# Attention scores on one core: first unit loaded contiguously and stored in halves, and a looped TensorE program over one 8-bank PSUM tensor

## The chip, the cores and the metric

The kernel runs on one core of a Trainium2 chip. The metric is the device time of one execution in microseconds, given as the median over nine executions. The engines are named as in the profile: PE is TensorE, DVE is VectorE, ACT is ScalarE, POOL is GpSimd, SP is SyncE. SP computes nothing here: it issues transfers to the core's 16 DMA engines.

## The reference

```python
batch, heads, seq, dim = 8, 8, 512, 64          # q, k: float32 [8, 8, 512, 64]
scale = 1.0 / np.sqrt(q.shape[-1])
return (np.einsum('bhqd,bhkd->bhqk', q, k) * scale).astype(np.float32)
```

There are 64 pairs of batch and head. Each one gives a 512 by 512 score matrix from a 512 by 64 query and a 512 by 64 key. The inputs hold 16.78 MB together, the output 67.11 MB.

## The kernel before

**Units and tiles.** The work is cut into four units (`v`, 0 to 3) of two batches each. A unit has a 2.1 MB load of k and one of q. From a unit come four tiles, so there are sixteen (`g`, 0 to 15). A tile is an SBUF buffer of 128 partitions by 2 by 8 by 512 float32 values, 4.19 MB, and is stored with one transfer. The index `x` (0 or 1) of the second dimension is one head of the two on each partition's row, called a half below; each half is 8 matmuls of 128 by 512.

**Buffers.** Three SBUF buffers `big0` to `big2` serve twice: the loads land in them (`xf`, line 58), and after the casts the tiles' results are written into them (`store_buffer`, line 62; tile g uses one of the three in turn). A tile can be filled only once the tile three before it, in the same buffer, has been stored.

**The engines' programs.** They are written out by hand and tied together by semaphores.

- SP (lines 69, 75, 91 to 102) issues the first half of the first k load (ACT issues the second half), then five loads, then the last two loads as buffers come free (`ready`). After that it loops over the tiles: it waits until ACT and DVE have written a tile, then issues its store (line 99). Each buffer has a semaphore of stores, `store_sems[g % 3]`; a store adds 16. At the end it waits for all stores.
- POOL (line 121) casts what was loaded to bf16 and counts `ready` up, once for each load.
- DVE (lines 148, 156) turns keys and queries with 32 by 32 block transposes into `kT` and `qz`: six transposes for one batch (`steps(b)`), which serves two tiles. The transposes of the next batch are laid between the PSUM evictions, by the table `after`.
- PE (line 140) does 256 matmuls. They are unrolled in the instruction stream, two for each of 128 pairs. A pair writes one of four PSUM buffers (`pss`, two banks each) in rotation, and before writing it PE waits until the pair four before has been taken out. At the second matmul of a tile PE also waits until its SBUF buffer is free: on `ready` for the first three tiles, and from the fourth on the semaphore of the store three tiles before.
- ACT and DVE (lines 186, 189) take each pair, 128 by 1024 values, out of PSUM, scale it and write it to the tile's buffer. `takers` says who takes which of the eight pairs of a tile: ACT five, DVE three.

**What the access patterns say.** `k_r`, `q_r` (lines 41, 42) and `out_r` (line 43) describe how DRAM rows lie on the partitions. In `out_r` the partition dimension `(h u)` is one head number and 64 row blocks; these lie one behind the other in DRAM, so that dimension is a single one of 128 steps, of 16 KB each. The store's pattern on the DRAM side is 128 by 2 by 4096 values, on the SBUF side too. The loads' pattern is 32 by 4 by 4096 on the DRAM side (the two half loads: 32 by 4 by 2048) and 128 by 4096 on the SBUF side.

Of the kernel before, what the change touches and what calls it, by code (L numbers as in the profile page):

```python
# [5 lines left out]
def kernel(  # L6
    tc: tile.TileContext,
    q: bass.AP,
    k: bass.AP,
    out: bass.AP,  # L10
):
    nc = tc.nc
    B, H, S, D = q.shape
    scale = 1.0 / (D ** 0.5)
    P = 128
    Q = 32
    UNITS = B // 2
    G = H // 2
    M = P // (2 * H)
    R = S // M  # L20
    J = R // 2
    RO = 8
    U = S // RO
    JJ = J // RO
    PAIRS = RO
    ALL = 2 * B

    f32 = mybir.dt.float32
    bf16 = mybir.dt.bfloat16
    mult = mybir.AluOpType.mult  # L30


    names = ["ready", "zeroed", "pe", "act", "dve"]
    sem = {name: nc.alloc_semaphore(name) for name in names}
    load_sems = [nc.alloc_semaphore(f"load{n}") for n in range(2 * UNITS)]
    halves = [load_sems[0], nc.alloc_semaphore("load0b")]
    store_sems = [nc.alloc_semaphore(f"store{n}") for n in range(3)]

    q_r = q.rearrange("(v b) (x s h) (m j) d -> v (s h m) (b x) (j d)", b=2, x=2, s=2, j=R)
    k_r = k.rearrange("(v b) (x s h) (m j) d -> v (s h m) (b x) (j d)", b=2, x=2, s=2, j=R)
    out_r = out.rearrange("(v b) (x s h) (u i) k -> v s b (h u) x (i k)", b=2, x=2, s=2, i=RO)

    bigs = [nc.alloc_sbuf_tensor(f"big{n}", [P, 2, RO, S], f32)[:] for n in range(3)]
    xb = nc.alloc_sbuf_tensor("xb", [P, 2 * UNITS, J, D, 2], bf16)[:]
    kT = nc.alloc_sbuf_tensor("kT", [P, 2 * G, S], bf16)[:]
    qz = nc.alloc_sbuf_tensor("qz", [P, 2 * G, RO, P], bf16)[:]
    pss = [nc.alloc_psum_tensor(f"ps{n}", [P, 2, S], f32)[:] for n in range(4)]

    xw = xb.rearrange("p n w d e -> p n (w d e)").bitcast(f32).rearrange(
        "p n (w d) -> p n w d", d=D)
    kw = kT.bitcast(f32)
    qw = qz.bitcast(f32)

    def xf(v):
        return bigs[(0, 1, 2, 1)[v]].rearrange("p x i k -> p (x i k)").rearrange(
            "p (x s c) -> p x s c", x=2, s=2)  # L60

    def store_buffer(g):
        return bigs[(0, 2, 1)[g % 3]]

    def rows(v, x):
        return (k_r, q_r)[x][v]

    def load(v, x):
        nc.sync.dma_start(out=xf(v)[:, x].rearrange("p s c -> p (s c)"), in_=rows(v, x)  # L69
                          ).then_inc(load_sems[2 * v + x], 16)  # L70

    for s, queue in enumerate((nc.sync, nc.scalar)):
        first_load = queue.dma_start(
            out=xf(0)[:, 0, s], in_=rows(0, 0)[..., s * R * D // 2:(s + 1) * R * D // 2]
        ).then_inc(halves[s], 16)
        tc.no_tile_sem_insts.add(first_load.ins.name)
    tc.close()
    tc.compile()  # L80


    takers = ["act", "dve", "act", "act", "dve", "act", "dve", "act"]

    def taken(pair):
        g, p = divmod(pair, PAIRS)
        who = takers[p]
        return who, g * takers.count(who) + takers[:p + 1].count(who)


    for n in range(1, 2 * (UNITS - 1)):
        load(n // 2, n % 2)
    for x in range(2):
        nc.sync.wait_ge(sem["ready"], 3 + x)
        load(UNITS - 1, x)
    for g in range(ALL):
        for who in ("act", "dve"):
            nc.sync.wait_ge(sem[who], takers.count(who) * (g + 1))
        nc.sync.dma_start(out=out_r[g // 4, g // 2 % 2, g % 2], in_=store_buffer(g).rearrange("p x i k -> p x (i k)")
                          ).then_inc(store_sems[g % 3], 16)  # L100
    for n in range(3):
        nc.sync.wait_ge(store_sems[n], 16 * len(range(n, ALL, 3)))


    for v in range(UNITS):
        for x in range(2):
            if v or x:
                nc.gpsimd.wait_ge(load_sems[2 * v + x], 16)
            for s in range(2):
                if v == x == 0:  # L110
                    nc.gpsimd.wait_ge(halves[s], 16)
                src = xf(v)[:, x, s]
                dst = xb[:, 2 * v + x]
                if x == 0:
                    src = src.rearrange("p (w e d) -> p w e d", e=2, d=D)
                    dst = dst[:, s * J // 2:(s + 1) * J // 2].rearrange("p w d e -> p w e d")
                else:
                    src = src.rearrange("p (jj e i d) -> p jj e i d", e=2, i=RO, d=D)
                    dst = dst.rearrange("p (i jj) d e -> p jj e i d", i=RO)[
                        :, s * JJ // 2:(s + 1) * JJ // 2]  # L120
                cast = nc.gpsimd.tensor_copy(out=dst, in_=src)  # L121
            cast.then_inc(sem["ready"], 1)


    pe = nc.tensor
    for pair in range(ALL * PAIRS):
        g, p = divmod(pair, PAIRS)
        n, i = g % 4 * 2 + p // 4, p % 4 * 2
        for w in range(2):
            if w == 0 and pair >= 4:  # L130
                who, count = taken(pair - 4)
                pe.wait_ge(sem[who], count)
            elif w == 0 and pair == 0:
                pe.wait_ge(sem["zeroed"], 2)
            if p == 0 and w == 1:
                if g < 3:
                    pe.wait_ge(sem["ready"], (2, 6, 8)[g])
                else:
                    pe.wait_ge(store_sems[g % 3], g // 3 * 16)
            ins = pe.matmul(out=pss[pair % 4][:, w, :], lhsT=qz[:, n, i + w], rhs=kT[:, n],  # L140
                            start=True, stop=True)
        ins.then_inc(sem["pe"], 1)

    def turn_keys(b, y):
        s = b % 2 * 2 * Q
        return nc.vector.transpose(  # L148
            out=kw[2 * y * Q:2 * (y + 1) * Q, b % 2 * G:(b % 2 + 1) * G].rearrange(
                "d g (m w) -> d w m g", w=J),  # L150
            in_=xw[s:s + 2 * Q, b // 2 * 2, :, y * Q:(y + 1) * Q])

    def turn_queries(b, y, h):
        s = (b % 2 * 2 + h) * Q
        d = (2 * y + h) * Q
        return nc.vector.transpose(  # L156
            out=qw[d:d + Q, b % 2 * G:(b % 2 + 1) * G, :, h * Q:(h + 1) * Q].rearrange(
                "d g i (m jj) -> d i jj m g", jj=JJ),
            in_=xw[s:s + Q, b // 2 * 2 + 1, :, y * Q:(y + 1) * Q].rearrange(
                "p (i jj) d -> p i jj d", i=RO))  # L160

    def steps(b):
        nc.vector.wait_ge(sem["ready"], b // 2 * 2 + 1)
        yield turn_keys(b, 0)
        yield turn_keys(b, 1)
        nc.vector.wait_ge(sem["ready"], b // 2 * 2 + 2)
        for y in range(2):
            for h in range(2):
                yield turn_queries(b, y, h)

    nc.vector.memset(qz, 0.0).then_inc(sem["zeroed"], 1)  # L171
    nc.vector.wait_ge(sem["zeroed"], 1)
    for last in steps(0):
        pass
    last.then_inc(sem["zeroed"], 1)


    after = {(0, 1): 1, (0, 4): 1, (0, 6): 2, (1, 1): 2}
    coming = iter(())
    for pair in range(ALL * PAIRS):  # L180
        g, p = divmod(pair, PAIRS)
        o = store_buffer(g)[:, p // 4, p % 4 * 2:p % 4 * 2 + 2, :]
        ps = pss[pair % 4]
        if takers[p] == "act":
            nc.scalar.wait_ge(sem["pe"], pair + 1)
            nc.scalar.mul(out=o, in_=ps, mul=scale).then_inc(sem["act"], 1)  # L186
        else:
            nc.vector.wait_ge(sem["pe"], pair + 1)
            nc.vector.tensor_scalar(out=o, in0=ps, scalar1=scale, scalar2=None, op0=mult  # L189
                                    ).then_inc(sem["dve"], 1)  # L190
        if p == 0 and g % 2 == 0 and g // 2 + 1 < 2 * UNITS:
            coming = steps(g // 2 + 1)
        for _ in range(after.get((g % 2, p), 0)):
            next(coming, None)


# [28 lines left out]
```

## Time and profile before

| | us |
|---|---|
| median of 9 executions | 201.64 (201.42 to 201.73) |
| the profiled execution, its own time | 201.71 |
| its span, first to last instruction | 200.4 |
| DVE busy | 155.0 |
| PE busy | 86.5 |
| ACT busy | 79.6 |
| POOL busy | 39.1 |

The span is what the trace covers; the execution's own time is 1.3 us longer. Busy times of the engines overlap each other. HBM traffic is 16.78 MB read and 67.11 MB written. The mean time of one instruction of each kind: a matmul 503 ns, an ACT eviction of 128 by 1024 1024 ns, a DVE eviction of the same size 1218 ns, a transpose of the keys 1946 ns and of the queries 2003 ns, a POOL cast 2468 ns. From issue to landing a store takes 15.2 us (median of 16).

### The profile page before, as it was taken

To read this page: it belongs to the slowest core of one execution; us is meant where nothing else is said; L and a number is where in the kernel's file an instruction comes from. 1 tells how busy PE (TensorE), PEld (TensorE's weight loads), DVE (VectorE), ACT (ScalarE), POOL (GpSimd) and SP (SyncE) were. 2 spreads that over 40 slices of the span, in tenths; PEclk is the share of its full clock that TensorE was granted. 3 is DMA by queue.
4 is the path that set the end of the run, shared out by engine and by line. 5 is a ranking of instruction groups with operands and counts; after the bars stand their busy time and mean duration, and the time that the engine had idled before them with its cause. 6 is when DMAs were issued, how large, how long until landed. Compare 5 with 4: busy or idle time off the path is not lost.

```text
span 200.4 us, 784 instructions
## 1 busy us (share of the span) xinstructions
PE 86.5 (43%) x251; PEld 28.3 (14%) x256; DVE 155.0 (77%) x97; ACT 79.6 (40%) x81; POOL 39.1 (19%) x20
## 2 busy tenths in 40 slices
PE   0000075464935492349225745573556247930000
PEld 0000021121311131113112211221122112300000
DVE  2338959995999899989998999899999996740000
ACT  2000036272852475327532942393347344860000
POOL 0489999986000000000000000000000000000000
PEclk9999999575797579856996975597578965885555
DMA  5999999999999999999999999999999999999996
GB/s 201 427 438 442 428 419 419 451 360 432 428 442 425 432 428 442 417 432 428 445 422 430 428 442 425 432 428 442 422 428 435 425 428 435 428 428 419 425 419 278
DMA packets 5652, 83.94 MB, mean 419 GB/s; under 512 B 400, under 2 KB 400, under 8 KB 400
## 3 DMA queue, kind: packets, MB, share of 16 engines
q1 hardware_dynamic: 5504, 82.84, 97.4%
q10 hardware_dynamic: 144, 1.05, 1.2%
q8 instruction: 2, 0.03, 0.1%
q14 instruction: 2, 0.02, 0.0%
HBM read 16.78 MB, written 67.11 MB: 419 GB/s over the span
## 4 chain that ended last, share of the span: by engine, by line
DVE 53%; DMA 17%; PE 8%; POOL 5%; ACT 3%; issue 1%; SPq 1%
DVE qz L156 24%; DVE big L189 18%; DMA big<-in_q_dram 17%; DVE kT L148 12%; PE ps L140 8%; POOL xb L121 5%; ACT big L186 3%; SPq L69 1%
## 5 line engine op out<-in xcount | busy, mean ns | idle before, releaser
L140 PE MATMUL ps<-kT,qz 128*128 128x512 bf16 x251 | 86.5, 503 | 90.7 <-DVE big L189 57.0
L186 ACT ACTIVATE big<-ps 128x1024 f32<-128x1024 f32 x80 | 78.3, 1024 | 96.1 <-PE ps L140 93.6
L189 DVE TENSOR_SCALAR big<-ps 128x1024 f32<-128x1024 f32 x48 | 57.8, 1218 | 11.1 <-PE ps L140 10.7
L156 DVE STREAM_TRANSPOSE qz<-xb 32x1024 f32<-32x1024 f32 x32 | 64.1, 2003 | 1.3 <-POOL xb L121 0.8
L140 PEld LDWEIGHTS ps<-kT,qz 128*128 128x128 bf16 x256 | 28.3, 121 | 148.4 <-DVE big L189 75.1
L121 POOL CAST xb<-big 128x2048 bf16<-128x2048 f32 x16 | 38.9, 2468 | 9.0 <-DMA big<-in_k_dram 7.9
L148 DVE STREAM_TRANSPOSE kT<-xb 64x1024 f32<-64x1024 f32 x16 | 31.1, 1946 | 6.8 <-POOL xb L121 6.4
L171 DVE MEMSET qz<- 128x4096 uint32 x1 | 3.5, 3472 | 3.5 <-PEq L80 3.5
L186 ACT ACT_TABLE_LOAD x1 | 1.3, 1283 | 2.6 <-PEq L80 2.6
L209 POOL MEMSET const-float32-0.0<- 128x1 f32 x1 | 0.1, 98 | 0.2 <-issue 0.2
L209 POOL MEMSET const-bfloat16-1.0<- 128x1 bf16 x1 | 0.1, 101 | 0.0
L209 POOL MEMSET const-uint8-127<- 128x1 uint8 x1 | 0.1, 101 | 0.0
L209 POOL MEMSET const-float32-1.0<- 128x1 f32 x1 | 0.1, 98 | 0.0
## 6 DMA issues: line engine op xcount, KB each, us to landing
out_dram<-big SPq DMA_DIRECT2D x16, 4096.0 KB, 15.2
big<-in_q_dram SPq DMA_DIRECT2D x4, 2048.0 KB, 17.3
big<-in_k_dram SPq DMA_DIRECT2D x3, 2048.0 KB, 14.9
big<-in_k_dram SPq DMA_DIRECT2D x1, 1024.0 KB, 5.7
big<-in_k_dram ACTq DMA_DIRECT2D x1, 1024.0 KB, 10.0
```

The costliest lines, as they stand in the source:

```text
L69: nc.sync.dma_start(out=xf(v)[:, x].rearrange("p s c -> p (s c)"), in_=rows(v, x)).then_inc(load_sems[2 * v + x], 16)
L121: cast = nc.gpsimd.tensor_copy(out=dst, in_=src)
L140: ins = pe.matmul(out=pss[pair % 4][:, w, :], lhsT=qz[:, n, i + w], rhs=kT[:, n], start=True, stop=True)
L148: return nc.vector.transpose(out=kw[2 * y * Q:2 * (y + 1) * Q, b % 2 * G:(b % 2 + 1) * G].rearrange("d g (m w) -> d w m g", w=J), in_=xw[s ...
L156: return nc.vector.transpose(out=qw[d:d + Q, b % 2 * G:(b % 2 + 1) * G, :, h * Q:(h + 1) * Q].rearrange("d g i (m jj) -> d i jj m g", jj=J ...
L171: nc.vector.memset(qz, 0.0).then_inc(sem["zeroed"], 1)
L186: nc.scalar.mul(out=o, in_=ps, mul=scale).then_inc(sem["act"], 1)
L189: nc.vector.tensor_scalar(out=o, in0=ps, scalar1=scale, scalar2=None, op0=mult).then_inc(sem["dve"], 1)
L209: nc = _bacc.Bacc("TRN2", target_bir_lowering=False, num_devices=1)
```

## The change

It has four parts.

1. **The first unit's layout.** For unit 0, `rows` now gives k and q of the first two batches as plain contiguous memory, 128 rows of 4096 values (the two half loads: 128 rows of 2048). A partition is now batch, head and eighth of the sequence, where it was head, eighth, batch and part of the heads. The transposes of the first two batches (`inside(b)`) therefore write their result in another order.
2. **The first unit's stores.** With that layout the two heads of a half are four apart in the output. A half is described by the new pattern `out_0`, in which `h` (2 steps of 4 MB) and `u` (64 steps of 16 KB) are two dimensions that can't be one. Each of tiles 0 to 3 is stored by two transfers, one for each half, of 2 by 64 by 4096 values on the DRAM side and 128 by 4096 on the SBUF side. Each adds 16 to the buffer's semaphore, so such a tile adds 32. Tiles 4 to 15 are stored as before.
3. **PSUM and the evictions.** PSUM is one tensor of 8 banks, and matmul i of a half always writes bank i. A half is taken out in three groups: banks 0 and 1 by DVE, 2 to 4 and 5 to 7 by ACT. There are 32 DVE evictions of 128 by 1024 (were 48) and 64 ACT evictions of 128 by 1536 (were 80 of 128 by 1024). DVE does two transposes after the eviction of three of every four halves, none after the fourth.
4. **PE's loop and the waits.** PE runs a loop of four iterations over four tiles (64 matmuls). [...] the semaphores come in two sets (`act0`, `act1`, `dve0`, `dve1`, `next0`, `next1`), which PE counts down again. Leave for a tile's SBUF buffer no longer comes from the store's own semaphore: SP passes it on. After it has issued tile g's store, SP waits for the store of tile g - 1 (for the buffer of tile g + 2) and adds one to `next0` or `next1`, and only then goes on to tile g + 1.

```diff
+    out_0 = out.rearrange("b (h t x) (u i) k -> b t x h u (i k)", h=2, x=2, i=RO)
     out_r = out.rearrange("(v b) (x s h) (u i) k -> v s b (h u) x (i k)", b=2, x=2, s=2, i=RO)
...
-    pss = [nc.alloc_psum_tensor(f"ps{n}", [P, 2, S], f32)[:] for n in range(4)]
+    ps = nc.alloc_psum_tensor("ps", [P, RO, S], f32)[:]
...
     def rows(v, x):
-        return (k_r, q_r)[x][v]
+        if v == 0:
+            return (k, q)[x][:2].rearrange("b g (m j) d -> (b g m) (j d)", j=R)
+        return (k, q)[x].rearrange(
+            "(v b) (x s h) (m j) d -> v (s h m) (b x) (j d)", b=2, x=2, s=2, j=R)[v]
...
-            out=xf(0)[:, 0, s], in_=rows(0, 0)[..., s * R * D // 2:(s + 1) * R * D // 2]
+            out=xf(0)[:, 0, s], in_=rows(0, 0)[:, s * R * D // 2:(s + 1) * R * D // 2]
...
+    groups = [(0, 2, "dve"), (2, 3, "act"), (5, 3, "act")]
+    share = {"act": 4, "dve": 2}
+    def stored(n, tiles):
+        return sum(32 if g < 4 else 16 for g in range(n, tiles, 3))
...
     for g in range(ALL):
         for who in ("act", "dve"):
-            nc.sync.wait_ge(sem[who], takers.count(who) * (g + 1))
-        nc.sync.dma_start(out=out_r[g // 4, g // 2 % 2, g % 2], in_=store_buffer(g).rearrange("p x i k -> p x (i k)")
-                          ).then_inc(store_sems[g % 3], 16)
+            nc.sync.wait_ge(sem[f"{who}{g // 2 % 2}"], share[who] * (g % 2 + 1))
+        o = store_buffer(g).rearrange("p x i k -> p x (i k)")
+        if g < 4:
+            for x in range(2):
+                nc.sync.dma_start(out=out_0[g // 2, g % 2, x], in_=o[:, x]
+                                  ).then_inc(store_sems[g % 3], 16)
+        else:
+            nc.sync.dma_start(out=out_r[g // 4, g // 2 % 2, g % 2], in_=o
+                              ).then_inc(store_sems[g % 3], 16)
+        for later in ((1, 2) if g == 0 else (g + 2,)):
+            if later < ALL:
+                if later < 3:
+                    nc.sync.wait_ge(sem["ready"], 4 + 2 * later)
+                else:
+                    nc.sync.wait_ge(store_sems[later % 3], stored(later % 3, later))
+                nc.sync.sem_inc(sem[f"next{later // 2 % 2}"], 1)
...
-    for pair in range(ALL * PAIRS):
...
-                    pe.wait_ge(store_sems[g % 3], g // 3 * 16)
-            ins = pe.matmul(out=pss[pair % 4][:, w, :], lhsT=qz[:, n, i + w], rhs=kT[:, n],
-                            start=True, stop=True)
-        ins.then_inc(sem["pe"], 1)
+    takes = {(0, 3): ("next", 2), (1, 3): ("dve", 2 * share["dve"]), (1, 6): ("act", 2 * share["act"])}
+    pe.wait_ge(sem["zeroed"], 2)
+    with pe.Fori(0, ALL // 4):
+        for t in range(4):
+            two, r = divmod(t, 2)
+            for x in range(2):
+                before = (2 * t + x - 1) % 8
+                for i in range(RO):
+                    if i in waits:
+                        who, count = waits[i]
+                        pe.wait_ge(sem[f"{who}{before // 4}"], before % 4 * per_half[who] + count)
+                    elif x == 0 and i == 1:
+                        pe.wait_ge(sem[f"next{two}"], r + 1)
+                    ins = pe.matmul(out=ps[:, i], lhsT=qz[:, 2 * t + x, i], rhs=kT[:, 2 * t + x],
+                                    start=True, stop=True)
...
+    def inside(b):
+        return "g m" if b < 2 else "m g"
...
-                "d g (m w) -> d w m g", w=J),
+                f"d g (m w) -> d w {inside(b)}", w=J),
...
-    after = {(0, 1): 1, (0, 4): 1, (0, 6): 2, (1, 1): 2}
...
+    for g in range(ALL):
+        for x in range(2):
+            for i, rows_, who in groups:
+                count += 1
+                engine = nc.scalar if who == "act" else nc.vector
+                engine.wait_ge(sem["pe"], count)
+                o, src = store_buffer(g)[:, x, i:i + rows_], ps[:, i:i + rows_]
...
+            for _ in range(2 if (g % 2, x) != (1, 1) else 0):
+                next(coming, None)
```

## The prediction

> **What bounds the kernel now.** I read the page's DMA rows first, then busy time by stretches, then SP's own waits, and last the queues' packet counts.
>
> The page (slices of 5.0 us; the busy row in tenths, then what was moved), and its section on queues:
>
> ```profile
> PE 86.5 (43%) x251; PEld 28.3 (14%) x256; DVE 155.0 (77%) x97; ACT 79.6 (40%) x81; POOL 39.1 (19%) x20
> DMA  5999999999999999999999999999999999999996
> GB/s 201 427 438 442 428 419 419 451 360 432 428 442 425 432 428 442 417 432 428 445 422 430 428 442 425 432 428 442 422 428 435 425 428 435 428 428 419 425 419 278
> DMA packets 5652, 83.94 MB, mean 419 GB/s; under 512 B 400, under 2 KB 400, under 8 KB 400
> ...
> q1 hardware_dynamic: 5504, 82.84, 97.4%
> q10 hardware_dynamic: 144, 1.05, 1.2%
> ...
> HBM read 16.78 MB, written 67.11 MB: 419 GB/s over the span
> ```
>
> The DMA engines are full in 38 of 40 slices, while no compute engine is busy more than 77% of the span. The transfers are the bound. Busy time by stretches (PE, weight loads, DVE, ACT, POOL, each with its count; then clock, DMA share, GB/s):
>
> ```profile
> 5.00:36.00 31.00, 6.67 (x17) 2.30 (x17) 21.67 (x13) 5.01 (x5) 27.43 (x12) 0.99 1.01 432
> 36.00:46.00 10.00, 5.61 (x15) 1.95 (x15) 9.91 (x6) 4.90 (x5) 9.12 (x5) 0.67 0.98 393
> ...
> 106.00:126.00 20.00, 11.34 (x31) 3.46 (x32) 18.99 (x13) 9.80 (x10) 0.00 (x0) 0.70 1.01 431
> 126.00:146.00 20.00, 10.96 (x32) 3.42 (x32) 18.97 (x14) 9.80 (x10) 0.00 (x0) 0.70 1.01 431
> ```
>
> With a share of 1.01 the 16 engines move 431 GB/s, so one moves 431/16 = 26.94 GB/s. Each carries 83.89/16 = 5.243 MB, which takes 194.6 us. The other 200.4 - 194.6 = 5.8 us are the start, the last landing, and a dip at 36 to 46 us worth (431 - 393)/431 x 10 = 0.9 us.
>
> The chain of waits names DVE for 53%, because DVE's instructions follow each other without gaps. It runs 97% full over two tiles (49.86 to 69.75 us in the chain, six evictions of 1.22 and six transposes of about 2.0 are 19.2 of 19.9). Two tiles' stores are 8.39 MB, or 19.5 us at 431 GB/s. DVE and DMA are level, with the loads' backlog in front of the DMA engines, and SP's waits show it:
>
> ```profile
> SPq L98 <- DVE big L189: 142.5, 16, 11.2
> SPq L69 <- POOL xb L121: 21.6, 2, 17.3
> SPq L102 <- DMA out_dram<-big: 21.6, 2, 19.3
> ```
>
> SP waits for DVE before each store, yet after the last store it still waits 19.3 us for the landing: two tiles were queued. Faster compute alone can therefore win only part of the 5.8 us.
>
> **The packet counts** carry most of what follows. Queue q1 has 16 stores of 128 x 2 rows and 8 loads of 128 rows, 4096 + 1024 = 5120 data packets. The 384 left are 24 transfers x 16. Queue q10 has one half load: 144 = 128 + 16. So each transfer of before ends with 16 small packets, one for each of 16 engines, and each engine has a sixteenth of its bytes.
>
> [...] The trace agrees for what it has: 128 against 128 and 32 against 128 both give 16, the 16 small packets. It has no transfer with a small outer dimension. [...]
>
> **The change part by part.**
>
> *Stores of tiles 0 to 3.* Before, 4 transfers with outer dimensions 128 and 128. After, 8 of 2.10 MB with 2 on the DRAM side and 128 on the SBUF side. [...] Bytes on each of these two:
> - loads: 16.78/16 = 1.049 MB;
> - tiles 0 to 3: 4 x 4.194/2 = 8.389 MB (were 1.049);
> - tiles 4 to 15: 12 x 4.194/16 = 3.146 MB.
>
> The sum is 12.583 MB, 2.4 times 5.243. At 26.94 GB/s that is 467.1 us. One of these tiles is 2.097 MB on each of the two engines, 77.8 us, where it took 9.7.
>
> Do the two engines ever run dry? The loads keep them to about 43 us (the last one landed at 43.4). Tile 0's store was issued at 35.9 and will queue behind them. Then SP issues tile 1, waits until tile 0 is stored, issues tile 2, and so on: one tile is always queued while one moves, and a tile is computed in about 10 us (tile 0 from the first matmul at 26.4 to its store at 35.9), long before 77.8 are over. I count tile 0 landing near 121, tile 1 near 199, 2 near 276 and 3 near 354. Tile 4 is issued at about 276, when tile 2 has landed. The other 14 engines finish their share of it in 10 us, the two do so only after tile 3, near 364. Then eleven tiles at 9.7 us follow in the same way. The overheads of before remain without the dip, 5.8 - 0.9 = 4.9 us: 467.1 + 4.9 = 472.0 us of span. The execution's time stood 1.3 above its span: 473.3. Its own time, 201.71, is 0.07 above the median of the runs, so 473.
>
> The unknown is the speed of one engine when fourteen are idle. Below: [...] the best slice of before, 451/16 = 28.2, gives 452. Above: the worst full stretch, 393/16 = 24.6, gives 512 + 6.2 = 518. I take 26.94, since it holds over a hundred microseconds, and each engine's packets were 16 KB rows before and stay so.
>
> *SP's added waits.* SP waits for tile g - 1's landing before it goes on to tile g + 1; behind it stand only the stores. In 16-engine work a store was issued 15.2 us before its landing and the tile before the previous one had landed 2 x 9.7 - 15.2 = 4.2 us earlier: the wait would be over already, cost 0, at most the chain's usual hop of 0.05 us, under a queue of 9.7 us. Under two engines this wait holds tile 2's store to tile 0's landing, with tile 1 still queued: 0 as well. Without that queued tile it would cost a compute time, 10 us a tile.
>
> *Contiguous first loads.* The same bytes in rows of 8 and 16 KB. Issues took 0.63 and 0.54 us. Gain 0 to 0.6 us at the start of tile 0, which is behind the loads on the DMA queues; I take 0. *Eight transposes with other steps:* 1.95 and 2.0 us each as before; were they half as long again, 12 x 1.0 us, the DMA queue of 77.8 us a tile covers it.
>
> *Evictions.* DVE loses 16 x 1.218 = 19.5 us. ACT goes from 80 x 1.024 to 64 of 1.5 times the size, at most 64 x 1.54 = 98.3 us. PE has the same 256 matmuls. *PE's loop:* three branches taken; [...] hidden for the same reason. All of it: 0.
>
> **Rivals.**
>
> - *Stores spread over 16 engines all the same* (not slower). For it: every transfer of before, also 32 against 128, ran on 16. [...] Then bytes per engine are as before, 194.6 us. DVE over two tiles: three halves of 1.22 + 4.0 and a fourth bound by PE and ACT near 3.5, 19.2 us, against 19.9 before and 19.5 for the DMA. Some of the dip and tail would go: 0.9 + 0.3, about 200.5. It decides as soon as k is 8 or more: at k = 8 the two-fold share of four tiles, 1.05 MB, adds 39 us to eight of the engines, still slower; so only k = 16 ends here.
> - *Each half on its own pair of engines*, four in all. For it: two transfers for a tile. [...] 1.049 + 4.194 + 3.146 = 8.389 MB, 311.4 + 6.2 = 318 us.
> - *The new PSUM handoff or the loop becomes the bound* with 16-engine stores: if the fourth half took 5.2 us too, 20.9 us for two tiles, 8 x 1.0 more, 209. It needs the first rival's condition.
>
> **How the numbers follow.** Two engines: 0.92, 473 us, own range 440 to 510. Sixteen: 0.05, of it 0.02 faster, 0.015 within, 0.015 slower. Four: 0.03. A measurement of this kernel tells a change of about 0.2% from none. Slower: 0.92 + 0.03 + 0.015 = 0.965; within 0.015; faster 0.02. The range of the likeliest case is the whole one, cut at the top to 510, since the 393 GB/s stretch mixed a gap into its mean.
>
> **What would show it.** Packets in q1: with k = 2 they are 8 x 130 + 12 x 272 + 8 x 144 = 5456, with k = 16 5568; under 512 B 352 against 464. From about 45 to 350 us the DMA row should stand at one tenth with some 54 GB/s, but for tile 4's burst on the other engines near 276, and then, for tiles 4 to 15, move at 431 or below. PE, ACT and DVE are idle for some 70 us between tiles. From issue to landing the half stores of tiles 0 to 2 should take 45 to 155 us. A DMA row that stays at nine makes this wrong at its first step; one tenth at another rate than 54 GB/s makes only the size wrong.

## The result, and the profile after

| | before | after |
|---|---|---|
| median, us | 201.6 (201.29 to 201.9, 30 runs beside it) | 474.36 (474.31 to 474.72, 10 runs) |
| profiled execution: own time / span, us | 201.71 / 200.4 | 474.3 / 473.0 |

The changed kernel takes 2.354 times as long as the kernel before, with a 95% interval of 2.352 to 2.355. Here and below two executions that were much slower than their like are left out: one of 378.3 us of the kernel before and one of 214.33 us of the kernel that stores one head from each of two queues.

These are lines of the page of the changed kernel. The 40 slices are now 11.8 us each, so a digit covers more than twice the time that it covered before.

```profile
PE 92.3 (20%) x252; PEld 29.5 (6%) x256; DVE 137.1 (29%) x81; ACT 90.1 (19%) x65; POOL 38.9 (8%) x20
...
DMA  8995111111111111111111163111118999999993
GB/s 331 434 427 252 55 53 55 53 55 53 55 53 55 53 55 53 55 53 55 53 55 53 53 269 139 54 54 54 54 53 364 423 425 440 421 425 421 439 424 168
DMA packets 5602, 83.90 MB, mean 177 GB/s; under 512 B 352, under 2 KB 352, under 8 KB 352
...
q1 hardware_dynamic: 5456, 82.84, 41.4%
q10 hardware_dynamic: 144, 1.05, 0.7%
```

The bytes are the same. What is new is the long row of ones: from the fifth slice to the thirtieth the 16 DMA engines are busy for one tenth on average and move 53 to 55 GB/s. The one exception is a burst at slices 24 and 25. The packet counts say why. Queue q1 had 5504 packets, 384 of them the small ones that end a transfer on each engine. With eight half stores in place of four stores, sixteen engines for each would have given 5568. It has 5456, and 352 small packets where there were 400: twelve stores and eight loads with 16 each on q1, one load with 16 on q10, and eight half stores with 2 each.

Busy times by stretches of the changed kernel (start and end, length, then PE, weight loads, DVE, ACT, POOL with counts, clock, DMA share, GB/s):

```profile
46.00:120.00 74.00, 4.71 (x17) 1.34 (x18) 10.81 (x7) 6.27 (x5) 1.92 (x1) 0.57 0.13 54
...
200.00:275.00 75.00, 4.23 (x12) 1.16 (x9) 8.59 (x5) 5.22 (x4) 0.00 (x0) 0.52 0.13 54
275.00:290.00 15.00, 5.46 (x16) 1.66 (x16) 6.50 (x4) 5.48 (x4) 0.00 (x0) 0.73 0.74 289
290.00:350.00 60.00, 0.00 (x0) 0.00 (x0) 0.00 (x0) 0.00 (x0) 0.00 (x0) 0.50 0.13 54
...
400.00:430.00 30.00, 16.81 (x50) 5.27 (x48) 27.15 (x17) 17.34 (x13) 0.00 (x0) 0.83 1.01 429
```

A share of 0.13 is two of sixteen. The two move 54 GB/s, so each moves 27.0. In 290 to 350 us no computing engine has one instruction. At 275 tile 4, which sixteen engines share, goes out: the other fourteen do their part (289 GB/s in the mean of that stretch) and are idle again. From 356 us on all sixteen work as before.

Two pieces from the chain of waits (start, length, what), and one row of SP's own waits:

```profile
48.08 29.66 SPq L106
77.74 0.05 issue
77.79 38.02 SPq L106
115.81 4.11 another core or an unknown queue
```

```profile
SPq L117 <- DMA out_dram<-big: 178.6, 13, 79.6
SPq L119 <- DMA out_dram<-big: 20.7, 2, 19.5
```

Line 106 is the issue of a half store. Tile 1's first half is issued at 48.08 us, and SP stands in that instruction for 29.66 us; in the second half it stands for 38.02 us. A store of before took 0.372 us to issue. Up to 300 us SP's waits for landings at line 117 are only 16.0 us in all; the longest, 79.6 us, is for tile 3 after tile 4's issue. The chain goes on after the tiles' landings: 119.9 us for tile 0, then 197.7, 275.4 and 356.0.

### The profile page after: what moved, and what is told of

The parts are those of the page before. It is cut to its first block, busy times and chain, and to the rows that moved or that the text cites. A ratio compares the mean times of both kernels' runs of the same rounds, so it can differ in the third digit from the quotient of the medians.

```text
span 473.0 us, 783 instructions
## 1 busy us (share of the span) xinstructions
PE 92.3 (20%) x252; PEld 29.5 (6%) x256; DVE 137.1 (29%) x81; ACT 90.1 (19%) x65; POOL 38.9 (8%) x20
## 3 DMA queue, kind: packets, MB, share of 16 engines
q1 hardware_dynamic: 5456, 82.84, 41.4%
## 4 chain that ended last, share of the span: by engine, by line
SPq 43%; another core or an unknown queue 22%; DMA 21%; POOL 5%; PE 2%; ACT 1%; issue 0%
SPq L106 43%; DMA out_dram<-big 16%; POOL xb L138 5%; DMA big<-in_k_dram 5%; PE ps L162 2%; ACT big L219 1%; SPq L109 0%; SPq L117 0%; SPq L102 0%
## 5 line engine op out<-in xcount | busy, mean ns | idle before, releaser
L162 PE MATMUL ps<-kT,qz 128*128 128x512 bf16 x252 | 92.3, 527 | 357.4 <-SPq L117 304.6
L219 ACT ACTIVATE big<-ps 128x1536 f32<-128x1536 f32 x64 | 88.8, 1451 | 359.8 <-PE ps L162 359.7
L221 DVE TENSOR_SCALAR big<-ps 128x1024 f32<-128x1024 f32 x32 | 39.2, 1224 | 299.8 <-PE ps L162 232.5
L162 PEld LDWEIGHTS ps<-kT,qz 128*128 128x128 bf16 x256 | 29.5, 125 | 419.7 <-SPq L117 307.9
```

What stands on the lines that cost most here:

```text
L162: ins = pe.matmul(out=ps[:, i], lhsT=qz[:, 2 * t + x, i], rhs=kT[:, 2 * t + x], start=True, stop=True)
L219: freed = engine.mul(out=o, in_=src, mul=scale)
L221: freed = engine.tensor_scalar(out=o, in0=src, scalar1=scale, scalar2=None, op0=mult)
```

## The experiments

Each kernel here differs from the kernel before or from the changed kernel in one part or two, which the heading or the text names. Each was run 2 to 20 times; their times stand beside 201.5 us for the kernel before, run with them.

### Stores by head instead of by half

The two transfers of tiles 0 to 3 are cut along the other dimension.

```diff
+    out_h = out.rearrange("b (h t x) (u i) k -> b t h u x (i k)", h=2, x=2, i=RO)
...
-            for x in range(2):
-                nc.sync.dma_start(out=out_0[g // 2, g % 2, x], in_=o[:, x]
+            for h in range(2):
+                nc.sync.dma_start(out=out_h[g // 2, g % 2, h], in_=o[h * U:(h + 1) * U]
```

> The changed kernel with tiles 0 to 3 stored by head: still two transfers of 2.10 MB for a tile with the same 16 KB rows, but 64 by 2 by 4096 on both sides, so that 64 and not 2 is the outermost dimension. Theory (outer dimension 2 puts a store on two DMA engines): sixteen engines again, 5.24 MB each, 199.5 to 202 us; queue q1 with 5568 packets. Rival A (the loop, SP's waits or the two transfers for a tile cost the time): stays above 400 us. Rival B (a store from only 64 partitions draws at half speed): four tiles at 19.5 instead of 9.7 us, about 240 us.

Measured: 234.27 us, 1.165 times before (1.162 to 1.168). Rows of its page, then stretches:

```profile
GB/s 235 441 434 423 442 414 442 324 245 183 251 268 194 276 270 251 251 290 239 366 438 428 434 425 423 434 424 431 428 428 423 425 425 431 423 431 425 428 394 87
DMA packets 5714, 83.90 MB, mean 361 GB/s; under 512 B 464, under 2 KB 464, under 8 KB 464
```

```profile
46.00:66.00 20.00, 11.31 (x31) 3.61 (x31) 15.86 (x10) 10.03 (x9) 2.55 (x2) 0.66 1.00 221
66.00:96.00 30.00, 8.04 (x20) 2.63 (x21) 11.39 (x8) 6.65 (x5) 0.00 (x0) 0.62 1.00 258
126.00:166.00 40.00, 23.96 (x67) 7.53 (x66) 34.39 (x22) 22.39 (x17) 0.00 (x0) 0.76 1.01 429
```

The main step holds: with 64 outermost there are 464 small packets, 16 for each transfer, and 240 of the 273 us lost are back. Rival A is out. But the theory's 199.5 to 202 us missed, and rival B came near: the DMA engines show a full share of 1.00 and yet move 221 to 258 GB/s while these stores run. A full share doesn't mean full rate. The reason is taken up further below.

### Everything but unit 0's layout and stores

Unit 0 is loaded and stored as in the kernel before; PE's loop, the 8-bank PSUM, the eviction groups and SP's handing on of buffers stay.

```diff
-        if v == 0:
-            return (k, q)[x][:2].rearrange("b g (m j) d -> (b g m) (j d)", j=R)
...
-        if g < 4:
-            for x in range(2):
-                nc.sync.dma_start(out=out_0[g // 2, g % 2, x], in_=o[:, x]
-                                  ).then_inc(store_sems[g % 3], 16)
```

> The changed kernel with unit 0 loaded and stored as in the kernel before; the PE loop, the 8-bank PSUM tensor, the three eviction groups and SP's passing on of the buffers stay. Theory: these parts cost nothing that the DMA queue does not hide, 199.5 to 202.5 us. Rival: the loop or the new handoff is a bound of its own, 205 to 215 us.

Measured: 201.17 us (201.08 to 201.36), 0.9983 of before (0.9976 to 0.9990). Its profile has 1.01 and 431 GB/s in the middle, like before:

```profile
106.00:126.00 20.00, 12.29 (x33) 3.88 (x32) 17.09 (x11) 10.98 (x9) 0.00 (x0) 0.67 1.01 431
```

Beside stores on sixteen engines, these parts of the change are worth 0.3 us. DVE's busy time falls from 155.0 to 137.6 us, and almost nothing follows from it, because the transfers were the bound.

### The old program with unit 0's layout

The kernel before, with unit 0's contiguous load, and its tiles stored by half (2 by 64) or by head (64 by 2, with the lines of the by-head edit above). PE waits for the stores itself, as it did.

```diff
+        if v == 0:
+            return (k, q)[x][:2].rearrange("b g (m j) d -> (b g m) (j d)", j=R)
         return (k_r, q_r)[x][v]
...
+        if g < 4:
+            for x in range(2):
+                nc.sync.dma_start(out=out_0[g // 2, g % 2, x], in_=o[:, x]
+                                  ).then_inc(store_sems[g % 3], 16)
```

> The kernel before with only unit 0's layout and the half stores of tiles 0 to 3 (2 by 64 by 4096) taken from the change; PE program, PSUM and evictions as before, and PE waits for the stores itself. Theory (bytes on two engines alone make the time): 12.58 MB on each of two engines, 468 to 478 us, as the changed kernel. Rival (SP's waits between the stores, which hold tile g + 1 back until tile g - 1 has landed, make part of it): below 440 us.

> The kernel before with unit 0 loaded contiguously and its tiles stored by head (64 by 2 by 4096); unrolled PE program and evictions as before. Theory: 200 to 202.5 us, as the kernel before; the contiguous first loads gain at most 0.6 us. Rival: stores from 64 partitions are slower, up to 240 us.

Measured: 478.9 us by half and 235.61 us by head (1.170 of before, 1.168 to 1.171). Unit 0's layout with its half stores, without the other parts of the change, makes all of the loss. So SP's new waits, which stand in the changed kernel, make none. This kernel is even 4.5 us above the changed one, and 0.9 us above its forecast. A part of that shows in its trace: between 380 and 390 us the DMA share falls to 0.88 (374 GB/s), and between 400 and 410 us to 0.93 (396 GB/s), while the chain of waits follows DVE; the changed kernel moves 421 and 441 GB/s there. Against 431 GB/s the two dips are worth about 2 us; the rest stays open. By head, the forecast of 200 to 202.5 us missed as it did in the changed kernel.

### One tile only

In the by-head kernel, tile 0 alone is stored by half.

```diff
+                if g == 0:
+                    nc.sync.dma_start(out=out_0[g // 2, g % 2, n], in_=o[:, n]
+                                      ).then_inc(store_sems[g % 3], 16)
```

> The changed kernel with only tile 0 stored in halves (2 by 64); tiles 1 to 3 by head (64 by 2). Theory: the two engines carry 5.243 + 2.097 - 0.262 = 7.078 MB, 262.7 + 6.2 = 269 us (265 to 273). Rival (the time comes from SP standing in issues [...]): [...] at most 205 us.

Measured: 301.52 us, where 265 to 273 were expected. The sum started from 201 us, but this kernel's other tiles are stored by head, and its own base is 234.27 us. Against that base one tile by half costs 67.3 us; (2.097 - 0.262)/26.94 gives 68.1. Its own by-head cost went away with it, about (234.27 - 201.48)/4 = 8.2 us, so some 7 us more were lost than that sum has. They show in the trace: from 170 to 185 us, in three stretches of 5 us, the share is 0.73, 0.15 and 0.44, which is 8.4 us of idle DMA engines, and PE waits 15.0 us there for SP to hand on a buffer.

The rival allowed 205 us at most, on the assumption that two half stores alone would not make SP stand. It didn't hold: with only two half stores ahead, SP still stood 29.84 us in the next issue, which began at 48.02 us, and the mean share from 40 to 78 us was 0.16 (70 GB/s), against 1.00 (219 GB/s) from 78 to 97 us. What speaks against it is the DMA share. While SP stands in the changed kernel's issues, the share stays at 0.13, so the two engines are never idle, and SP's standing can't add to their time.

The same question without any layout or by-head store: the kernel before, where only tile 0's store is cut into 64 transfers of two partitions.

```diff
+        for h in range(0, P, 2 if g == 0 else P):
+            r = slice(h, h + 2) if g == 0 else slice(0, P)
+            nc.sync.dma_start(out=out_r[g // 4, g // 2 % 2, g % 2][r], in_=o[r]
+                              ).then_inc(store_sems[g % 3], 16)
```

> The kernel before, its layout too, with only tile 0's store cut into 64 transfers of 2 rows (2 by 2 by 4096); all other stores as before. Theory (an outer dimension of 2 puts a store on two engines): these carry 5.243 + 2.097 - 0.262 = 7.078 MB, 262.7 + 6.2 = 269 us (265 to 275, with 64 issues of SP). Rival (a two-dimensional DRAM side, not the size 2 of the outer dimension, is what costs): 201 to 206 us.

Measured: 288.19 us, where 265 to 275 were expected. Stretches of it:

```profile
46.00:66.00 20.00, 6.45 (x17) 2.08 (x17) 12.82 (x9) 4.90 (x5) 1.85 (x1) 0.67 0.12 37
66.00:86.00 20.00, 0.00 (x0) 0.00 (x0) 0.00 (x0) 0.00 (x0) 0.00 (x0) 0.50 0.13 53
```

Two engines again, in the old layout, so that the outer dimension of 2 is the cause and the output's two distant heads are not. It cost 86.7 us, not 68. In the first 20 us the two moved 37 GB/s and not 54, which is (54 - 37) x 20/54 = 6.3 us. From 106 to 126 us, with a share of 0.96, all sixteen moved 360 GB/s and not 431, worth about 3 us; the remaining 9 us stay open.

### Another queue, and eight engines

In the kernel before with unit 0's layout, ACT issues the second half store of tiles 0 to 3 on its own queue, after its last eviction of the tile.

```diff
+            if g < 4 and p == PAIRS - 1:
+                for who in ("act", "dve"):
+                    nc.scalar.wait_ge(sem[who], takers.count(who) * (g + 1))
+                nc.scalar.dma_start(out=out_0[g // 2, g % 2, 1],
...
+                                    ).then_inc(store_sems[g % 3], 16)
```

> The kernel before with unit 0's layout, where SP issues the first half store of tiles 0 to 3 and ACT, on its own queue, the second (both 2 by 64). Theory [...]: 468 to 480 us. Rival (another queue, or another transfer, gets another pair): four engines with 8.389 MB each, about 318 us.

Measured: 477.78 us. The queues' rows and one stretch of its profile:

```profile
q1 hardware_dynamic: 4936, 74.45, 37.2%
q10 hardware_dynamic: 664, 9.44, 4.7%
```

```profile
46.00:120.00 74.00, 5.81 (x17) 1.96 (x17) 13.26 (x9) 4.81 (x5) 3.21 (x2) 0.57 0.13 54
```

ACT's queue has 144 + 4 x 130 = 664 packets, so the half stores ran there, and the share is still 0.13 at 54 GB/s. Two queues did not make four engines. The rival of different pairs (318 us) is out.

In the changed kernel, tiles 0 to 3 were also stored in pieces of 8 rows.

```diff
+            for h in range(2):
+                for u in range(0, U, 8):
+                    nc.sync.dma_start(out=out_h[g // 2, g % 2, h, u:u + 8],
+                                      in_=o[h * U + u:h * U + u + 8]
+                                      ).then_inc(store_sems[g % 3], 16)
```

> The changed kernel with tiles 0 to 3 stored in sixteen pieces of 8 rows (8 by 2 by 4096 on both sides, 262 KB). Theory (8 engines for an outer dimension of 8): 1.049 + 2.097 + 3.146 = 6.292 MB on each of eight engines, 233.6 + 6.2 = 240 us (236 to 248, the 64 issues of SP included). Rival (any outer dimension below 16 falls to two or fewer engines): above 450 us. Rival (sixteen engines for it too): about 202 us.

Measured: 254.76 us. The stretch in which these stores run:

```profile
56.00:106.00 50.00, 9.63 (x28) 3.05 (x28) 15.88 (x10) 9.53 (x8) 0.00 (x0) 0.60 0.50 200
```

A share of 0.50 is eight engines, as the theory has it. They moved 200/8 = 25.0 GB/s each and not 26.94, which makes 2.097 MB longer by 6 us of the 15 that the forecast lacked. From 46 to 56 us they moved 167 GB/s, which is worth another 2 us; the other 7 stay open.

### Why sixteen engines were not enough

By head, a transfer takes its rows from 64 neighbouring partitions, and these stores moved 221 to 258 GB/s at a share of 1.00. The theory from here on is that the range of partitions sets this rate. If half of the partitions gave half of 431, that would be 215 GB/s, which is my estimate. The measured 221 to 258 lies up to a fifth above it; the next store, from the other half, may already run beside the end of one, which no run shows apart. Four runs tested it. The first two keep the old layout and cut the stores of tiles 0 to 3 in two, by partitions or by `x`.

```diff
+            r = slice(h * U, (h + 1) * U) if g < 4 else slice(0, P)
+            nc.sync.dma_start(out=out_r[g // 4, g // 2 % 2, g % 2][r], in_=o[r]
...
+            r = slice(h, h + 1) if g < 4 else slice(0, 2)
+            nc.sync.dma_start(out=out_r[g // 4, g // 2 % 2, g % 2][:, r], in_=o[:, r]
```

> The kernel before, its layout too, with the stores of tiles 0 to 3 cut by partitions: rows 0 to 63 and rows 64 to 127, each 64 by 2 by 4096. Theory now [...]: as the by-head kernels, 230 to 238 us, DMA share full at 215 to 280 GB/s while these stores run. Rival (the contiguous layout's DRAM side, 4 MB between heads, is slow): 200 to 203 us.

> The kernel before with the stores of tiles 0 to 3 cut by x: two transfers of 2.10 MB as well, but each from all 128 partitions (128 by 4096). Theory (partitions count, not the number or size of the transfers): 201 to 202.5 us. Rival (2.10 MB stores, or two for a tile, are slow in themselves): 230 to 238 us.

Measured: 236.35 us with 64 rows (1.170, 1.164 to 1.176) and 201.5 us with 128 (0.9995, 0.9987 to 1.0004). Both have two stores of 2.10 MB for a tile, 464 small packets, and the old layout. Stretches of the one with 64 rows, and the page's rate row of the one with 128:

```profile
46.00:56.00 10.00, 5.67 (x17) 1.83 (x17) 7.75 (x7) 4.79 (x5) 2.13 (x1) 0.83 0.94 203
56.00:66.00 10.00, 5.19 (x14) 1.95 (x15) 9.39 (x6) 4.12 (x5) 0.00 (x0) 0.66 1.02 226
```

```profile
GB/s 198 430 438 445 425 419 419 438 370 429 435 425 435 432 435 427 429 422 438 422 438 427 438 425 429 429 435 432 432 429 432 429 432 432 429 432 425 435 429 262
```

So it is the partitions that a store takes its rows from. The distance in DRAM is not the cause: the full stores of the kernel before take the same two blocks per partition, 4 MB apart, and move 431 GB/s. The third run has both halves of the partitions in transfer at once: head 0 from SP's queue, head 1 from ACT's. Its first forecast is for two ranges whose rates add up, the rival's for rates that don't. The edit is that of the second half on ACT's queue, with `out_h` and `[U:]`.

> The kernel before with unit 0's layout, tiles 0 to 3 stored by head, head 0 (partitions 0 to 63) from SP's queue and head 1 (64 to 127) from ACT's[...]. [...] 201 to 212 us. Rival [...]: 230 to 238 us.

Measured: 211.17 us (1.047, 1.043 to 1.051). Its stretches:

```profile
46.00:56.00 10.00, 6.68 (x18) 2.46 (x20) 6.22 (x6) 4.29 (x5) 3.60 (x2) 0.66 1.02 311
56.00:66.00 10.00, 3.64 (x14) 0.96 (x13) 9.91 (x7) 5.13 (x6) 0.00 (x0) 1.00 0.98 375
```

The same stores from two queues move 311 to 375 GB/s: more than the 215 estimated for 64 partitions, less than 431. In stretches of 5 us the rate swings from 213 to 413 GB/s. Why it doesn't stay at the top was not tested. The last run is the edit with pieces of 8 rows with 16 in place of 8, so that each piece should have sixteen engines; its first forecast is for a limit by partitions.

> The changed kernel with tiles 0 to 3 stored in eight pieces of 16 rows (16 by 2 by 4096, 524 KB). [...] 230 us or more[...]. Rival (only the number of engines counts): 201 to 205 us.

Measured: 240.34 us, slightly above the by-head kernel, as a limit by partitions has it: in stretches of 10 us from 46 to 116 us, 193 to 275 GB/s at a share of 0.88 to 0.99. The pieces of 8 rows fit too. Eight engines moved 200 GB/s there; sixteen, which take a head's 64 partitions in one store, moved 221 to 258. Twice the engines brought little.

That the range of partitions limits the stores is shown by these runs: 236.35 us with 64 rows, 201.5 with 128. What lies behind it was not shown.

## Why the prediction was right

The time was forecast at 473 us, measured at 474.36. By its steps:

- **Two engines for the half stores.** Right, but the trace of before did not show it: it has no transfer with an outer dimension below 32. The counts forecast for k = 2, where k is the number of engines that a transfer runs on, 5456 packets in q1 and 352 under 512 B, are the counts of the page. The runs with 8 rows (share 0.50) and with two rows in the old layout (0.13) show that the size of the outermost dimension sets it. That both queues use the same two engines is shown by the half stores on ACT's queue (0.13 and 54 GB/s); which two of the sixteen they are, no run shows.
- **12.583 MB on each of the two at 26.94 GB/s.** Right: 27.0 GB/s each with fourteen engines idle. They were neither faster nor slower than beside the others, which was the unknown that made the range wide; its low end of 440 us, for faster engines than any stretch of before shows, was not reached. The loss of 272.8 us is 68.2 us for each of four tiles; the sum had 68.1.
- **They never run dry.** Right. Forecast landings of tiles 0 to 3: 121, 199, 276, 354. The chain goes on at 119.9, 197.7, 275.4 and 356.0, and after tile 4's landing at 365.7, forecast at 364. Tile 4's burst came at 275, and ACT waited 67 to 75 us between tiles.
- **Overheads of 4.9 and 1.3 us.** Span forecast 472.0, measured 473.0; its own time is again 1.3 us above it. That it came within 1 us is in part luck: the same sum holds for the old program with half stores, whose profiled span was 477.7.
- **All other parts at zero.** Beside stores on sixteen engines right within 0.3 us, PE's loop with its branches among them, by the run without unit 0's part. Beside the half stores they gained 4.5 us, 474.36 against 478.9, which the forecast had at nothing; that is 1% of the time. No run takes the contiguous first loads alone. Two figures of the forecast are off without weight: the transposes that write in another order are twelve, as its sum has it, not eight, and 64 x 1.54 is 98.6. An ACT eviction of 128 by 1536 took 1451 ns, below the bound of 1540, and DVE's busy time fell by 17.4 us in that run (forecast: 19.5) with no more gain than those 0.3 us.
- **SP's wait at zero.** Right: the half stores alone, without SP's waits, cost as much. But the picture of SP was incomplete. I had it wait for landings; up to tile 4 the trace has it standing in the issues, up to 38.2 us each, with little left to wait for a landing. SP's wait isn't free everywhere: with one tile by half, PE waited 15.0 us for SP's leave.
- **The first rival, half stores on sixteen engines at about 200.5 us,** didn't occur, but nothing speaks against its size: half stores from all 128 partitions on sixteen engines, in the old layout, took 201.5 us. What was mis-sized is my expectation of the first experiment, 199.5 to 202 us by head. It took the number of engines for the whole condition, and storing by head, the plain mend, gives 234. The new layout puts a head on 64 partitions, and every store of it that was tried is either two heads in two dimensions (two engines) or one head or a part of it (64 partitions or fewer).

The version without unit 0's part beats both kernels, by 0.17% of the time before.

## What to carry to other kernels

Before a transfer's pattern is changed, read the outermost dimension that is left on both sides: here two DRAM blocks that were no longer neighbours turned 128 into 2 by 64, and the transfer fell from sixteen DMA engines, with 431 GB/s, to two, with 54. In these profiles the count of the small packets per transfer, 16 or 2, gave the number of engines, and a busy share that stayed at a fixed fraction with idle compute, 0.13, confirmed it. Check the partitions as well: sixteen engines on 64 partitions showed a share of 1.00 at 221 to 258 GB/s, where 128 partitions had 431, so read share and GB/s together.

## What was not expected of the hardware

- SP stood in the issue of a half store for up to 38.2 us (median of the eight 33.4 us), against 0.372 us for a store on sixteen engines. The second halves of tiles 1 to 3 were released at 115.81, 192.31 and 268.81 us, 4.1 to 6.5 us before the tile ahead of each had landed, so when the half store two places ahead was nearly out. My estimate from these times is that about two half stores could be issued and not yet landed before SP stood in the next issue; what sets that number was not shown.
- A DMA engine that the trace shows as busy can be slow: in the by-head kernel the share is 1.00 at 221 GB/s.
- Two queues with 64 partitions each reached 311 to 375 GB/s, not 431.
